# One ring of raw staging tiles from the output projection to the FFN, and the first FFN weights loaded and summed within the last attention pair

## The chip, the cores and the metric

The kernel runs on one NeuronCore of a Trainium2 chip. TensorE (PE) does the matmuls, VectorE (DVE), ScalarE (ACT) and GpSimd (POOL) the rest, and SyncE (SP) issues most of the DMA transfers; ACT issues some. The metric is the device time of one execution in microseconds (us).

## What is computed

One encoder layer on x of 2048 positions by 1024 channels, in fp32:

```python
h = _rmsnorm(x, norm_mix_g)
x = x + _hybrid_mixer(h, ...)              # gMLP, pooling and dilated attention heads, then y @ w_out
h = _rmsnorm(x, norm_mem_g)
x = x + _memory_cross_attention(h, mem_n, w_q, w_kv, w_o, b_o)   # 4 heads, 256 memory tokens
h = _rmsnorm(x, norm_ffn_g)
x = x + _conv_ffn(h, ...)                  # up to 2 x 2816, width-3 convolution, silu gate, down
return _rmsnorm(x, final_norm_g)
```

## The kernel before

**Number format.** Each fp32 operand is kept as a high part, which the matmul takes exactly, and a low part, the rest. `mm3` makes a product of three matmuls: high by high (L115), high by low (L116), low by high (L117). So each weight that is loaded must be split: one operation makes the high part (POOL in `split_w`, ACT in the FFN), one on DVE the low part.

**Stages.** The order in time is: input projection and mixer; output projection in four chunks of 512 positions (`OutProj.chunk`); cross-attention (`xattn`); FFN up for the first half of the positions (`up_half(0)`); FFN down and up for the rest.

**Output projection.** A chunk loads six `y` tiles, splits them, and for each of eight blocks d of output channels loads `xt`, does 18 matmuls into `pt`, adds on DVE (L1265), and writes x1 to DRAM. During chunks 2 and 3 the eight row blocks of the matrix `a_d` (for the logits) are loaded through staging tiles `st` and split into `am0` to `am7`. The pool of `st`, `c_st`, has two buffers.

**Cross-attention.** The eight row blocks of `vo_d` (values times output weights) go through the same two `st` buffers and are split into `vm0` to `vm7`; POOL makes the high parts (L95), DVE the low parts (L99). `logits(s)` treats 128 positions: x1 is loaded and split, 48 matmuls go into `pl`, DVE takes the maximum `mx` (L1347) and scales it to `nm`, ACT takes exponentials into `p` (L1350), POOL divides. `ssq` (L1321) is the sum of squares for the norm, which PE adds over partitions (`pr`, L74). `turn` transposes `p` on DVE (L108, 16 operations). Two such blocks are a pair: `parts` splits the transposed `p` into `ph` and `pl_`, and `pv` does, for each of eight d, 24 matmuls into `po` (two PSUM buffers), an addition on DVE (`xr`, L1400), a DMA of x2 to DRAM, a square on ACT and its addition on POOL (`sq`, in the last pair `sql`, L1407). `xr` has three buffers, and the buffer of the square only one.

**FFN.** The up product is done with seven block products instead of eight (a Strassen-like scheme): from two loaded weight tiles `wa` and `wb`, POOL makes sums and differences `ws` and `wt` with four operations (L272 to L277), and `split` makes high parts on ACT (L265) and low parts on DVE (L266). `prep(0)` makes the matching sums of the activations (`hb`) and their parts `hth`, `htl`, for four groups kk. It is a generator, advanced between the steps of the last two attention pairs; its last piece, for kk = 3, comes after the last `pv`, since the pool `f_h3` is opened only there. The FFN starts with

```python
self.w0 = self.weights(self.ORDER[0])
rest()
```

The first products are `px`, `pz` and `py`.

**What sets the order.** Each engine works its own instructions in program order and waits on semaphores. The program order on each engine is laid down when the kernel is built, by a scheduler that simulates the program; memory comes from pools, and a tile that takes over the space of an older tile waits for whatever still uses it. So a change of pools moves instructions on all engines.

Of the kernel before, what the change touches and what calls it, by code (L numbers as in the profile page):

```python
# [9 lines left out]
F32 = mybir.dt.float32  # L10
# [109 lines left out]
class Ffn:  # L120
# [13 lines left out]
    def __init__(self, cx, es, x2, w_up, b_up, conv, w_down, b_down, gn, g_fin, act, out):  # L134
# [4 lines left out]
        self.pool = cx.pools(es)  # L139
# [11 lines left out]
    def open(self):  # L151

        one = self.one = self.pool("f_one", 1, side="right")
        self.carry = one.tile([P, 2 * NF, 3], F32, name="carry")
        self.h3 = self.pool("f_h3", 1, side="right")
        self.raw = self.pool("f_raw", 5, side="right")
        self.wp = self.pool("f_w", 1, side="right")

    def prep(self, half, es):
# [37 lines left out]
        for kk in range(4):  # L197
# [29 lines left out]
            else:  # L227
                sub(dve, T1, B12, B11)
                sub(gps, T3, B22, B12)
                sub(dve, T2, B22, T1)  # L230
                yield
# [3 lines left out]
                sub(gps, T4, B21, T2)  # L235
# [8 lines left out]

    def weights(self, fa):

# [4 lines left out]

    def weight_pieces(self, fa, w):

        nc, N, raw = self.nc, self.N, self.raw
        a = raw.tile([P, 2, N], F32, name="wa", tag="raw")
        nc.sync.dma_start(a.rearrange("p a n -> p (a n)"), self.w_up[fa])
        b = raw.tile([P, 2, N], F32, name="wb", tag="raw")
        nc.sync.dma_start(b.rearrange("p a n -> p (a n)"), self.w_up[fa + 1])
        s = raw.tile([P, 2, N], F32, name="ws", tag="raw")
        t = raw.tile([P, 2, N], F32, name="wt", tag="raw")  # L260

        def split(src, prods):
            m = len(prods)
            hl = self.wp.tile([P, 2, m, N], F32R, name="w", tag=f"w{m}", bufs=4 if m == 2 else 2)
            nc.scalar.activation(hl[:, 0], src, AF.Copy)  # L265
            nc.vector.tensor_tensor(hl[:, 1], src, hl[:, 0].bitcast(F32), op=ALU.subtract)  # L266
            for j, p in enumerate(prods):
                w[p] = (hl[:, 0, j], hl[:, 1, j])

        split(a, (1, 2))  # L270
        tt = nc.gpsimd.tensor_tensor
        tt(s[:, 0], b[:, 0], b[:, 1], op=ALU.add)  # L272
        tt(s[:, 1], s[:, 0], a[:, 0], op=ALU.subtract)
        yield
        split(s, (5, 6))
        tt(t[:, 0], a[:, 0], b[:, 0], op=ALU.subtract)
        tt(t[:, 1], a[:, 1], s[:, 1], op=ALU.subtract)  # L277
        split(t, (7, 3))
        split(b[:, 1:2], (4,))
# [240 lines left out]

    def run(self, rest, sq):
# [3 lines left out]
        self.w0 = self.weights(self.ORDER[0])  # L525
        rest()

# [4 lines left out]
        with ExitStack() as e:  # L532
            pool, pst, pu = banks(e, 1)
            self.up_half(0, pu, pool, lambda: cx.rows_of(self.one, pst, sq, 2, cx.r3[:, NS - 2:], 1.0))
            for c0 in (0, N):
                pt = pst.tile([P, N], F32, name="pt", tag="pt")
                cx.spread(self.one, pt, cx.r3[:, (H + c0) // P:(H + c0 + N) // P])
                nc.scalar.activation(cx.rb[:, c0:c0 + N], pt, AF.Copy)  # L538
# [684 lines left out]
class OutProj:  # L1223


    def __init__(self, cx, late, es, eo, x_t, yt, w_out, b_out, x1_d):
        self.cx, self.x_t, self.yt, self.x1_d = cx, x_t, yt, x1_d
        pool = cx.pools(es)
        self.st = pool("c_st", 2, side="right")
# [11 lines left out]
    def load_w(self, pl, tag, src, st=None):  # L1241
        t = (st or self.st).tile([P, D], F32, name="st", tag="st")
# [28 lines left out]
def xattn(cx, proj, es, eo, a_d, vo_d, b_o, x1_d, x2_d, ffn):  # L1271
# [6 lines left out]
    with es:  # L1278
# [91 lines left out]
        def parts(pts, spare):  # L1370

            if spare:
                ph = [proj.st.tile([P, 4, N2], F32R, name="ph2", tag="st") for _ in range(2)]
                pl = [pw.tile([P, 4, N2], F32R, name="pl2", tag="pt", bufs=2) for _ in range(2)]
            else:
                ph = wk.tile([P, KD, N2], F32R, name="ph", tag="ph", bufs=1)
                pl = wk.tile([P, KD, N2], F32R, name="pl_", tag="pl_", bufs=1)
                ph, pl = ([t[:, :4], t[:, 4:]] for t in (ph, pl))  # L1380
# [43 lines left out]
        for q in range(NS // 2):  # L1424
# [6 lines left out]
            elif q == last - 1:  # L1431
# [7 lines left out]
                def each(d):  # L1439
                    if d == 2:  # L1440
                        nxt.append(turn_pe(p2))
                    if d > 1 and len(nf[0].hs) < 3:
# [98 lines left out]
```

## Time and profile before

| | us |
|---|---|
| time, median of 3 runs | 2560.48 (2557.45 to 2561.59) |
| the profiled execution, its own time | 2568.14 |
| its span, first to last instruction | 2566.3 |
| PE busy in it | 2477.1 (97%) |
| DVE, ACT, POOL busy | 1807.6, 1000.3, 959.3 |

PE is busy nearly all the time. What a change can win is mostly idle time of PE, and time in which PE ran at the lower of its two clock levels. The profiled execution is 7.7 us longer than the median.

### The profile page before, as it was taken

How to read it: one execution, taken by the hardware profiler on the slowest of the kernel's cores; microseconds unless marked ns; L12 is line 12 of the kernel's file. 1: busy time of each engine (PE TensorE's matmuls, PEld its weight loads, DVE VectorE, ACT ScalarE, POOL GpSimd, SP SyncE). 2: the span in 40 equal slices, each digit the busy share in tenths (PEclk: the TensorE clock that was granted, in tenths of full speed). 3: DMA queues.
4: the chain of work that ended last, by engine and by line, in shares of the span. 5: the costliest groups of instructions: out<-in, count | busy, mean ns of one | idle time of the engine just before them, and what ended most of it. 6: DMA issues, size and time to landing. Idle time of an engine off the chain costs nothing. (4 is left out here: it accounts for less than half of the span.)

```text
span 2566.3 us, 34002 instructions
## 1 busy us (share of the span) xinstructions
PE 2477.1 (97%) x12454; PEld 2115.8 (82%) x12454; DVE 1807.6 (70%) x2658; ACT 1000.3 (39%) x1524; POOL 959.3 (37%) x805
## 2 busy tenths in 40 slices
PE   8999997899999999998999999999999999999998
PEld 6998896898877899987888888877888887888886
DVE  6575747777655876777888888786888887645553
ACT  4122112566311333333444444453444444444442
POOL 3212314674102333346555554025565553111000
PEclk9999998899999999999999999999999999999998
DMA  9345527675663122133222223582222223867673
GB/s 300 115 141 153 152 69 222 205 235 177 195 215 122 58 68 73 52 104 110 83 74 91 82 74 107 191 266 91 84 74 83 90 74 107 277 216 240 211 233 119
DMA packets 220096, 361.59 MB, mean 141 GB/s; under 512 B 38828, under 2 KB 104472, under 8 KB 219928
## 3 DMA queue, kind: packets, MB, share of 16 engines
q1 hardware_dynamic: 155980, 286.83, 35.6%
q10 hardware_dynamic: 63948, 72.58, 8.3%
q8 instruction: 98, 1.61, 0.3%
q14 instruction: 70, 0.57, 0.1%
HBM read 280.61 MB, written 79.90 MB: 140 GB/s over the span
## 5 line engine op out<-in xcount | busy, mean ns | idle before, releaser
L403 DVE TENSOR_TENSOR w<-dr,w 128x1024 fp32r<-128x1024 f32 x176 | 220.0, 1258 | 167.4 <-ACT w L402 163.7
L116 PE MATMUL pd<-w 128*128 128x512 f32 x704 | 274.5, 390 | 1.7 <-DVE w L403 1.7
L117 PE MATMUL pd<-w 128*128 128x512 f32 x704 | 274.1, 389 | 0.0
L402 ACT ACTIVATE w<-dr 128x1024 fp32r<-128x1024 f32 x176 | 185.0, 1058 | 216.9 <-PE pd L117 198.8
L115 PE MATMUL pd<-w 128*128 128x512 f32 x704 | 259.2, 390 | 0.7 <-ACT rb L538 0.7
L116 PE MATMUL py<-htl,w 128*128 128x512 f32 x528 | 208.5, 395 | 0.0
L115 PE MATMUL py<-hth,w 128*128 128x512 f32 x528 | 207.0, 394 | 0.8 <-DVE u L371 0.8
L117 PE MATMUL py<-hth,w 128*128 128x512 f32 x528 | 206.0, 394 | 0.0
L315 DVE SCALAR_TENSOR_TENSOR t<-u,vec,t 128x1022 f32<-128x1022 f32 (+1 forms) x88 | 134.0, 1523 | 70.0 <-ACT t L314 48.1
L314 ACT ACTIVATE t<-u,vec 128x1022 f32<-128x1022 f32 (+1 forms) x88 | 109.5, 1244 | 158.3 <-DVE u L364 139.6
L116 PEld LDWEIGHTS pd<-w 128*128 128x128 f32 x704 | 132.2, 188 | 30.0 <-DVE w L403 2.8
L115 PEld LDWEIGHTS pd<-w 128*128 128x128 f32 x704 | 132.0, 188 | 27.9 <-ACT rb L538 0.9
L117 PEld LDWEIGHTS pd<-w 128*128 128x128 f32 x704 | 132.2, 188 | 27.2
L115 PE MATMUL px<-hth,w 128*128 128x512 f32 x352 | 139.9, 397 | 6.5 <-ACT w L265 4.7
L95 POOL TENSOR_SCALAR wth<-st 128x1024 fp32r<-128x1024 f32 (+1 forms) x48 | 50.0, 1042 | 257.0 <-PE pz L116 174.9
L117 PE MATMUL px<-hth,w 128*128 128x512 f32 x352 | 139.5, 397 | 3.1 <-DVE w L266 3.1
L462 POOL TENSOR_TENSOR q<-q 128x512 f32<-128x512 f32 x24 | 38.4, 1598 | 274.7 <-ACT q L458 273.4
L116 PE MATMUL px<-htl,w 128*128 128x512 f32 x352 | 140.0, 398 | 0.0
L116 PE MATMUL pz<-htl,w 128*128 128x512 f32 x352 | 139.0, 395 | 0.0
L117 PE MATMUL pz<-hth,w 128*128 128x512 f32 x352 | 138.8, 394 | 0.0
L115 PE MATMUL pz<-hth,w 128*128 128x512 f32 x352 | 138.5, 393 | 0.0
L316 DVE SCALAR_TENSOR_TENSOR t<-u,vec,t 128x1022 f32<-128x1022 f32 (+1 forms) x88 | 136.2, 1548 | 0.1
(716 smaller groups left out, 7151.8 us busy)
## 6 DMA issues: line engine op xcount, KB each, us to landing
dr<-act_d SPq DMA_DIRECT2D x176, 256.0 KB, 3.8
dr<-in_w_down_dram SPq DMA_DIRECT2D x176, 256.0 KB, 4.1
wa<-in_w_up_dram SPq DMA_DIRECT2D x44, 512.0 KB, 3.2
wb<-in_w_up_dram SPq DMA_DIRECT2D x44, 512.0 KB, 3.3
st<-in_w_t_dram SPq DMA_DIRECT2D x32, 512.0 KB, 4.0
xt<-in_x_t_dram SPq DMA_DIRECT2D x56, 256.0 KB, 4.6
act_d<-t ACTq DMA_DIRECT2D x22, 513.0 KB, 3.1
act_d<-t ACTq DMA_DIRECT2D x22, 511.0 KB, 3.0
```

The lines of the kernel that those rows point to most:

```text
L95: nc.gpsimd.tensor_scalar(hi, src, 1.0, 1.0, op0=ALU.mult, op1=ALU.mult)
L115: mm(out, a[0], b[0], start=start, stop=False, skip_group_check=again)
L116: mm(out, a[0], b[1], start=False, stop=False, skip_group_check=again)
L117: self.mm = mm(out, a[1], b[0], start=False, stop=stop, skip_group_check=again)
L314: nc.scalar.activation(t, u[:, 1:n + 1], AF.Identity, bias=vec[:, 4, f:f + 1], scale=vec[:, 2, f:f + 1])
L315: nc.vector.scalar_tensor_tensor(t, u[:, 0:n], vec[:, 1, f:f + 1], t, op0=ALU.mult, op1=ALU.add)
L316: nc.vector.scalar_tensor_tensor(t, u[:, 2:n + 2], vec[:, 3, f:f + 1], t, op0=ALU.mult, op1=ALU.add)
L402: nc.scalar.activation(hl[:, 0], t, AF.Copy)
L403: nc.vector.tensor_tensor(hl[:, 1], t, hl[:, 0].bitcast(F32), op=ALU.subtract)
L462: nc.gpsimd.tensor_tensor(sq[0], sq[0], q, op=ALU.add)
```

## The change

The ring `raw` of five buffers (each 4 KB per partition) is opened with the output projection, in place of `c_st` (two buffers), of `f_raw` (five buffers, FFN) and of the single-buffered tiles for `ph` and `pl_`. Through it go, in this order, the loads of `a_d` and `vo_d`, the parts `ph` and `pl_` of the attention pairs (four of the five buffers each), and the FFN's weights. The load of the first FFN weights and POOL's four sums are issued in the last attention pair, after its second d (`stage_first`). The two spreads of the norm's row factors into `rb`, which stood behind `up_half(0)`, are done within it (`between`). In the last pair each step of `prep` is taken one by one, in a fixed number per d.

```diff
-        self.raw = self.pool("f_raw", 5, side="right")
...
+    def load(self, tile, fa, i):
+        self.nc.sync.dma_start(tile.rearrange("p a n -> p (a n)"), self.w_up[fa + i])
+        return tile
...
+    def sums(self, a, b, s, t):
+        tt = self.nc.gpsimd.tensor_tensor
+        tt(s[:, 0], b[:, 0], b[:, 1], op=ALU.add)
+        tt(s[:, 1], s[:, 0], a[:, 0], op=ALU.subtract)
+        tt(t[:, 0], a[:, 0], b[:, 0], op=ALU.subtract)
+        tt(t[:, 1], a[:, 1], s[:, 1], op=ALU.subtract)
...
+    def stage_first(self):
+        a, b, s, t = self.staged = [self.raw.tile([P, 2, self.N], F32, name="w" + n, tag="raw") for n in "abst"]
+        self.load(a, self.ORDER[0], 0)
+        self.load(b, self.ORDER[0], 1)
+        self.sums(a, b, s, t)
...
-        self.w0 = self.weights(self.ORDER[0])
+        (a, b, s, t), self.w0 = self.staged, {}
+        self.weight_part(self.w0, a, 1, 2)
+        self.weight_part(self.w0, s, 5, 6)
         rest()
+        self.weight_part(self.w0, t, 7, 3)
+        self.weight_part(self.w0, b[:, 1:2], 4)
...
-            self.up_half(0, pu, pool, lambda: cx.rows_of(self.one, pst, sq, 2, cx.r3[:, NS - 2:], 1.0))
-            for c0 in (0, N):
-                pt = pst.tile([P, N], F32, name="pt", tag="pt")
-                cx.spread(self.one, pt, cx.r3[:, (H + c0) // P:(H + c0 + N) // P])
-                nc.scalar.activation(cx.rb[:, c0:c0 + N], pt, AF.Copy)
+            def between():
+                cx.rows_of(self.one, pst, sq, 2, cx.r3[:, NS - 2:], 1.0)
+                for c0 in (0, N):
+                    pt = pst.tile([P, N], F32, name="pt", tag="pt")
+                    cx.spread(self.one, pt, cx.r3[:, (H + c0) // P:(H + c0 + N) // P])
+                    nc.scalar.activation(cx.rb[:, c0:c0 + N], pt, AF.Copy)
+            self.up_half(0, pu, pool, between)
...
-        self.st = pool("c_st", 2, side="right")
...
-        t = (st or self.st).tile([P, D], F32, name="st", tag="st")
+        t = (st or self.cx.raw).tile([P, D], F32, name="st", tag="st" if st else "raw")
...
+            def ring(n):
+                return cx.raw.tile([P, 4, N2], F32R, name=n, tag="raw")
             if spare:
-                ph = [proj.st.tile([P, 4, N2], F32R, name="ph2", tag="st") for _ in range(2)]
-                pl = [pw.tile([P, 4, N2], F32R, name="pl2", tag="pt", bufs=2) for _ in range(2)]
+                ph = [pw.tile([P, 4, N2], F32R, name="ph", tag="p"), ring("ph")]
+                pl = [pw.tile([P, 4, N2], F32R, name="pl_", tag="pt", bufs=2) for _ in range(2)]
             else:
-                ph = wk.tile([P, KD, N2], F32R, name="ph", tag="ph", bufs=1)
-                pl = wk.tile([P, KD, N2], F32R, name="pl_", tag="pl_", bufs=1)
-                ph, pl = ([t[:, :4], t[:, 4:]] for t in (ph, pl))
+                ph, pl = ([ring(n) for _ in range(2)] for n in ("ph", "pl_"))
...
                 def each(d):
-                    if len(nf[0].hs) < 3:
+                    for _ in range((1, 1, 1, 2, 1, 1, 1, 0)[d]):
                         next(pieces)
+                    if d == 1:
+                        nf[0].stage_first()
...
+            cx.raw = late.enter_context(tc.tile_pool(name="raw", bufs=5, side="right", reuse_waits="tile"))
```

**The SP queue in the second and third chunk.** `st<-vo_d` is a load of a row block of `vo_d`, `st<-a_d` of `a_d`; `xt` are the residual tiles of the chunks and `x1` the blocks for the logits. Before:

```order
L1261 DMA xt_7234<-in_x_t_dram 128x512
L1243 DMA st_7662<-a_d_98 128x1024
L1313 DMA x1_8158<-x1_d_100 128x8x128
L1243 DMA st_7714<-a_d_98 128x1024
L1261 DMA xt_7257<-in_x_t_dram 128x512
L1243 DMA st_7766<-a_d_98 128x1024
L1261 DMA xt_7280<-in_x_t_dram 128x512
L1243 DMA st_7818<-a_d_98 128x1024
L1261 DMA xt_7372<-in_x_t_dram 128x512
L1243 DMA st_7844<-vo_d_99 128x1024
L1261 DMA xt_7395<-in_x_t_dram 128x512
L1243 DMA st_7850<-vo_d_99 128x1024
```

After, the stretch up to the same `xt_7257`:

```order
L1260 DMA st_7766<-a_d_98 128x1024
L1260 DMA st_7818<-a_d_98 128x1024
L1260 DMA st_7844<-vo_d_99 128x1024
L1260 DMA st_7850<-vo_d_99 128x1024
L1330 DMA x1_8042<-x1_d_100 128x8x128
L1260 DMA st_7856<-vo_d_99 128x1024
L1330 DMA x1_8158<-x1_d_100 128x8x128
L1278 DMA xt_7211<-in_x_t_dram 128x512
L1260 DMA st_7862<-vo_d_99 128x1024
L1260 DMA st_7868<-vo_d_99 128x1024
L1278 DMA xt_7234<-in_x_t_dram 128x512
L1278 DMA xt_7257<-in_x_t_dram 128x512
```

Five loads of `vo_d` now stand ahead of `xt_7257`; before, none did, two came later in the chunk, and the other six behind the last chunk, where three stand now. Of the eight loads of `a_d`, five instead of two are now issued during the first chunk (not shown).

**DVE in the first two logits blocks.** `mx_8123` is the maximum of the second block, `vm6l` and `vm7l` are low parts of `vo_d`, and the transposes are those of the first block. Before:

```order
L108 STREAM_TRANSPOSE pt_8025<-p_8006 32x8x32 x15
L99 TENSOR_TENSOR vm6l_7883<-st_7880,vm6h_7882 128x1024
L108 STREAM_TRANSPOSE pt_8025<-p_8006 32x8x32
L1347 TENSOR_REDUCE mx_8123<-pl_8053 128x2
L99 TENSOR_TENSOR vm7l_7889<-st_7886,vm7h_7888 128x1024
L1348 TENSOR_SCALAR nm_8124<-mx_8123,r_7936 128x2
L1385 TENSOR_TENSOR pl__8258<-pt_8025,ph_8257 128x4x128 x2
L1321 TENSOR_REDUCE ssq_8662<-sx_8661 128x128
L1352 RECIPROCAL rd_8126<-dn_8125 128x2
L1347 TENSOR_REDUCE mx_8123<-pl_8053 128x2
L1348 TENSOR_SCALAR nm_8124<-mx_8123,r_7936 128x2
```

After:

```order
L108 STREAM_TRANSPOSE pt_8025<-p_8006 32x8x32 x16
L1364 TENSOR_REDUCE mx_8123<-pl_8053 128x2
L1365 TENSOR_SCALAR nm_8124<-mx_8123,r_7936 128x2
L1403 TENSOR_TENSOR pl__8259<-pt_8025,ph_8257 128x4x128
L1403 TENSOR_TENSOR pl__8260<-pt_8025,ph_8258 128x4x128
L1369 RECIPROCAL rd_8126<-dn_8125 128x2
L1364 TENSOR_REDUCE mx_8123<-pl_8053 128x2
L1365 TENSOR_SCALAR nm_8124<-mx_8123,r_7936 128x2
L1338 TENSOR_REDUCE ssq_8664<-sx_8663 128x128
```

The splits of `vm4` to `vm7` have gone from the first two blocks: those up to `vm6l` now stand ahead of the first block's maximum, and `vm7l` right behind it.

**ACT and POOL at the start of the FFN.** The rows are those behind the last attention product; `hth` and `htl` are parts of the activations, `s1` the last square, `w_12136` and `w_12157` the parts of the first weight tile `wa`. ACT before:

```order
L182 ACTIVATE hth_12158<-hb_12152 128x512
L1401 DMA x2_d_101<-xr_12077 128x256 [waits DMAHW2_49,DVE_49]
L1406 ACTIVATE s1_12106<-xr_12077 128x256 [waits Pool_49]
L265 ACTIVATE w_12136<-wa_12130 128x1024 [waits DMAHW0_49]
L265 ACTIVATE w_12149<-wb_12132 128x512 [waits DMAHW1_49]
L265 ACTIVATE w_12141<-ws_12134 128x1024 [waits Pool_49]
```

ACT after:

```order
L181 ACTIVATE hth_12163<-hb_12069 128x512
L1419 DMA x2_d_101<-xr_12108 128x256 [waits DMAHW3_49,DVE_49]
L1424 ACTIVATE s1_12137<-xr_12108 128x256 [waits Pool_49]
L260 ACTIVATE w_12157<-wa_11911 128x1024 [waits DMAHW4_49,DMAHW3_49,DMAHW5_49,DMAHW2_49,DMAHW6_49,DMAHW1_49,DMAHW7_49,DMAHW0_49,Pool_49]
L260 ACTIVATE w_12160<-ws_11913 128x1024
L260 ACTIVATE w_12174<-wt_11914 128x1024
L260 ACTIVATE w_12177<-wb_11912 128x512
```

The first weight operation of ACT waited for the load of `wa` alone; now it waits for the last writes of x2 (the eight DMA semaphores) and for POOL's last addition of a square, since its tile `w` takes over space that `xr` and the squares used. POOL before, from the first `sql` addition on:

```order
L1407 TENSOR_TENSOR sql_11823<-sql_11823,s1_11890 128x256
L1407 TENSOR_TENSOR sql_11823<-sql_11823,s1_11926 128x256
L1407 TENSOR_TENSOR sql_11823<-sql_11823,s1_11964 128x256
L1407 TENSOR_TENSOR sql_11823<-sql_11823,s1_11999 128x256
L1407 TENSOR_TENSOR sql_11823<-sql_11823,s1_12038 128x256
L1407 TENSOR_TENSOR sql_11823<-sql_11823,s1_12074 128x256
L185 TENSOR_TENSOR htl_12159<-hb_12152,hth_12158 128x1024
L1407 TENSOR_TENSOR sql_11823<-sql_11823,s1_12106 128x256
L272 TENSOR_TENSOR ws_12134<-wb_12132 128x512
L276 TENSOR_TENSOR wt_12135<-wa_12130,wb_12132 128x512
```

POOL after:

```order
L251 TENSOR_TENSOR ws_11913<-wb_11912 128x512
L253 TENSOR_TENSOR wt_11914<-wa_11911,wb_11912 128x512
L252 TENSOR_TENSOR ws_11913<-ws_11913,wa_11911 128x512
L187 TENSOR_TENSOR hb_12069<-hb_12069 128x512
L254 TENSOR_TENSOR wt_11914<-wa_11911,ws_11913 128x512
L187 TENSOR_TENSOR hb_12069<-hb_12069 128x512
L1425 TENSOR_TENSOR sql_11838<-sql_11838,s1_11904 128x256
L1425 TENSOR_TENSOR sql_11838<-sql_11838,s1_11950 128x256
L1425 TENSOR_TENSOR sql_11838<-sql_11838,s1_11988 128x256
L1425 TENSOR_TENSOR sql_11838<-sql_11838,s1_12030 128x256
```

The four sums have gone from behind the last `sql` addition to ahead of the first one. On PE the order behind the last attention product was two matmuls of `px`, then the other ten; now it is two of `px`, two of `pz`, two of `py`, then the other ten of `px`.

On all engines other rows are in another order too: on PE the two orders part at row 2,205 of some 12,300, in the mixer's attention, and last differ at row 9,001, in the FFN; the matmuls with weights are the same in number.

## Rows read from the trace of the kernel before

**Rows 1.** The page: span, busy time of the engines, one group of matmuls.
```profile
span 2566.3 us, 34002 instructions
PE 2477.1 (97%) x12454; PEld 2115.8 (82%) x12454; DVE 1807.6 (70%) x2658; ACT 1000.3 (39%) x1524; POOL 959.3 (37%) x805
...
L115 PE MATMUL pd<-w 128*128 128x512 f32 x704 | 259.2, 390 | 0.7 <-ACT rb L538 0.7
```

**Rows 2.** The waits of PE, 625 to 1200 us: waiting line, releaser, sum, times, longest.
```profile
PE px L115 <- ACT w L265: 4.7, 1, 4.7
PE pt L1018 <- ACT yo L1070: 4.1, 1, 4.1
```

**Rows 3.** Windows: length, busy PE, PEld, DVE, ACT, POOL, PE clock, DMA share, GB/s.
```profile
831.00:838.00 7.00, 4.89 (x12) 3.94 (x13) 6.40 (x21) 2.15 (x5) 4.20 (x5) 0.51 0.00 0
1186.00:1196.00 10.00, 5.03 (x11) 3.54 (x12) 7.66 (x4) 3.36 (x6) 9.92 (x8) 0.51 0.32 110
635.00:640.00 5.00, 5.00 (x21) 4.52 (x22) 3.27 (x8) 4.80 (x15) 0.00 (x0) 0.50 0.86 259
690.00:706.00 16.00, 13.87 (x64) 11.41 (x62) 8.23 (x8) 4.64 (x5) 6.03 (x4) 1.00 0.93 263
```

**Rows 4.** Timelines, SP queue and POOL: start, length, engine, line; in brackets idle before, releaser.
```profile
796.85 8.88 SPq L1243 DMA_DIRECT2D st<-vo_d  x4
...
800.90 1.05 POOL L95 TENSOR_SCALAR vm2h<-st 128x1024 fp32r<-128x1024 f32 x1 [5.23 <-DMA st<-vo_d]
819.39 1.05 POOL L95 TENSOR_SCALAR vm7h<-st 128x1024 fp32r<-128x1024 f32 x1 [1.53 <-DMA st<-vo_d]
```

**Rows 5.** Timelines of DVE and PE, 815 to 838 us.
```profile
824.49 1.23 DVE L99 TENSOR_TENSOR vm6l<-st,vm6h 128x1024 fp32r<-128x1024 f32 x1
826.21 0.69 DVE L1347 TENSOR_REDUCE mx<-pl 128x2 f32<-128x512 f32 x1
826.93 1.22 DVE L99 TENSOR_TENSOR vm7l<-st,vm7h 128x1024 fp32r<-128x1024 f32 x1
829.40 1.86 DVE L1321 TENSOR_REDUCE ssq<-sx 128x128 f32<-128x1024 f32 x1
...
831.32 0.59 PE L74 MATMUL pr<-ones,ssq 128*128 128x2 f32 x2 [2.47 <-DVE ssq L1321]
833.69 0.79 PE L115 MATMUL pl<-am0h,hh 128*128 128x512 f32 x1 [1.78 <-ACT p L1350]
```

**Rows 6.** Timelines of ACT, POOL, DVE and PE, 1181 to 1193 us.
```profile
1186.78 1.04 ACT L265 ACTIVATE w<-wa 128x1024 fp32r<-128x1024 f32 x1
...
1181.81 0.74 POOL L1407 TENSOR_TENSOR sql<-sql,s 128x256 f32<-128x256 f32 x1 [1.81 <-ACT s L1406]
1187.14 2.24 POOL L1407 TENSOR_TENSOR sql<-sql,s 128x256 f32<-128x256 f32 x1
1191.01 2.25 POOL L276 TENSOR_TENSOR wt<-wa,wb 128x512 f32<-128x512 f32 x1
...
1186.15 3.78 DVE L185 TENSOR_TENSOR htl<-hb,hth 128x1536 fp32r<-128x1536 f32 x2 [1.19 <-ACT hth L182]
1189.85 2.28 DVE L266 TENSOR_TENSOR w<-wa,w 128x1024 fp32r<-128x1024 f32 x1
...
1192.18 0.80 PE L117 MATMUL px<-hth,w 128*128 128x512 f32 x1 [3.09 <-DVE w L266]
```

**Rows 7.** Timelines of DVE and PE in the last attention pair.
```profile
1159.82 1.85 DVE L185 TENSOR_TENSOR htl<-hb,hth 128x1536 fp32r<-128x1536 f32 x1 [0.62 <-ACT hth L182]
1170.97 0.48 DVE L1400 SCALAR_TENSOR_TENSOR xr<-po,bo,xr 128x256 f32<-128x256 f32 x1
...
1171.51 0.38 PE L115 MATMUL po<-ph,vm0h 128*128 128x256 f32 x1
```

**Rows 8.** Timelines of the SP queue and of DVE, second chunk.
```profile
704.89 0.91 SPq L1261 DMA_DIRECT2D xt<-in_x_t_dram  x2
...
724.04 0.75 DVE L1265 SCALAR_TENSOR_TENSOR xt<-pt,bo,xt 128x512 f32<-128x512 f32 x1
```

More of the change, by code (lines that the diff above doesn't have):

```diff
@@ L138, in __init__ @@
         nc = self.nc
-        self.pool = cx.pools(es)
+        self.pool, self.raw = cx.pools(es), cx.raw
         self.eh = ExitStack()
@@ L230, in prep @@
                 sub(dve, T2, B22, T1)
+                sub(gps, T4, B21, T2)
                 yield
@@ L234, in prep @@
                 low(dve, B11, B12)
-                sub(gps, T4, B21, T2)
                 high(B21, B11)
@@ L243, in prep, with weight_part, weight_pieces @@
             self.hs.append((hi, lo))
+    def load(self, tile, fa, i):
[7 more added lines that the diff above has]
+        tt(t[:, 1], a[:, 1], s[:, 1], op=ALU.subtract)
+    def weight_part(self, w, src, *prods):
+        nc, N, m = self.nc, self.N, len(prods)
+        hl = self.wp.tile([P, 2, m, N], F32R, name="w", tag=f"w{m}", bufs=4 if m == 2 else 2)
+        nc.scalar.activation(hl[:, 0], src, AF.Copy)
+        nc.vector.tensor_tensor(hl[:, 1], src, hl[:, 0].bitcast(F32), op=ALU.subtract)
+        for j, p in enumerate(prods):
+            w[p] = (hl[:, 0, j], hl[:, 1, j])
+    def weight_pieces(self, fa, w):
+        a, b, s, t = (self.raw.tile([P, 2, self.N], F32, name="w" + n, tag="raw") for n in "abst")
+        self.load(a, fa, 0)
+        self.load(b, fa, 1)
+        self.weight_part(w, a, 1, 2)
+        self.sums(a, b, s, t)
+        yield
+        self.weight_part(w, s, 5, 6)
+        self.weight_part(w, t, 7, 3)
+        self.weight_part(w, b[:, 1:2], 4)
     def weights(self, fa):
@@ L250, in weights @@
         return w
[L252 to L279, printed above, removed]
     ORDER = [f + v for f in range(0, NF, 2) for v in (0, NF)]
@@ L519, in final @@
                                                                         x3[:, d - 1:d + 1])
+    def stage_first(self):
+        a, b, s, t = self.staged = [self.raw.tile([P, 2, self.N], F32, name="w" + n, tag="raw") for n in "abst"]
+        self.load(a, self.ORDER[0], 0)
+        self.load(b, self.ORDER[0], 1)
+        self.sums(a, b, s, t)
     def run(self, rest, sq):
         cx, nc, N, H = self.cx, self.nc, self.N, self.H
-        self.w0 = self.weights(self.ORDER[0])
+        (a, b, s, t), self.w0 = self.staged, {}
+        self.weight_part(self.w0, a, 1, 2)
+        self.weight_part(self.w0, s, 5, 6)
         rest()
+        self.weight_part(self.w0, t, 7, 3)
+        self.weight_part(self.w0, b[:, 1:2], 4)
         def banks(e, n):
@@ L1441, in each @@
                         nxt.append(turn_pe(p2))
-                    if d > 1 and len(nf[0].hs) < 3:
+                    if d > 1:
                         next(pieces)
```

## Prediction

> **What bounds the kernel now.** I read the page first: PE is busy 2477.1 us of a span of 2566.3, or 97% [rows 1]. The change adds and removes no matmul of weight, so it can win only where PE waits, or where it runs at the lower of its two clock levels, 1.2 instead of 2.4 GHz. Then I read the waits of PE and the timelines around them. Three places bear on the change.
>
> At the seam into the FFN PE waits 4.7 us for the first high part of a weight [rows 2], does two matmuls, and waits 3.09 us for the low part [rows 6]. From 1186 to 1196 us the granted clock is 0.51, the lower level [rows 3].
>
> In the first logits blocks of the cross-attention PE waits 2.47 us for `ssq` and, one small matmul later, 1.78 us for ACT's exponentials [rows 5]; behind that come 7 us at a clock of 0.51 [rows 3]. What is late there is DVE: between the transposes of the first block and the second block's maximum (826.21) stands `vm6l`, and right behind that maximum `vm7l`, 1.23 and 1.22 us, since `vo_d` came late: its loads are issued one by one from 796.85 on, over 8.88 us for the first four, and the split of the last begins at 819.39 [rows 4, 5].
>
> Ahead of the output projection PE waits 4.1 us for `yo` [rows 2], and 635 to 640 us run at 0.50 [rows 3]. The order of rows there changes too.
>
> **The change part by part.**
>
> *Loads of vo_d (ring of five).* After the change three loads instead of six are left when chunk 3 ends. Each needs one buffer free, that is one low part done on DVE. By the first such load, which is issued at 796.85 and whose split starts at 800.90 [rows 4], a load takes 4.05 us to its use. Buffers come free about every 1.2 us, so the last of the three is split by about 805, before the first maximum, where it was 819.39. Then DVE has no split left between the transposes and the second block. Taking away `vm6l` (1.23) moves the maximum from 826.21 to about 824.9. From that maximum to PE's next `pl` at 833.69 there are 7.48 us of work on DVE and ACT; out of it go `vm7l` (1.22) and `ssq` (1.86, at 829.40 [rows 5]), which now stands behind the second scaling, and which PE no longer needs here: the one `pr` left is for an earlier block. So PE can go on at 824.9 + 7.48 - 1.22 - 1.86, about 829.3 instead of 833.69, which I round to 4.2 us. Then the 7 us at half clock fall away. PE was busy 4.89 us in them [rows 3], and at full clock that work takes half: 2.4 us. Sum **-6.6**. Lower bound of the gain: the 4.2 us less the 1.7 of the second wait that may stay, -2.5 with the clock still falling. Upper bound: -9, if the waits on `xr` behind these blocks shrink too, which I do not count.
>
> *Seam.* The four sums and the loads are gone from here, and two high parts come one after the other on ACT. But the first high part now waits for the last addition of a square on POOL and the last writes of x2, where it waited for `wa` alone. That addition ended at 1189.38 (1187.14 plus 2.24), while the high part had started at 1186.78 [rows 6]. Nothing in the change brings this addition forward: in front of it stands the same `htl` on POOL, and beside it the same `htl` on DVE. So the high part starts at 1189.4 instead of 1186.78, and PE's first `px` at 1190.4, 2.6 us later than before. Then it pays back: two `px`, the next high part at 1191.5, and four matmuls of `pz` and `py` cover the low part, which DVE (free from 1189.93) has done by 1191.8. PE runs without a break from about 1191.5 with two matmuls done; before, that was 1192.18 [rows 6]. Gain 0.7. If the addition took 0.74 us as the one at 1181.81 did, it would end at 1187.9, and the gain were 2.2. Taken between: **-1.3**. Bounds: +2 if the writes of x2 land 2.7 us later than the addition (the weight loads that stood beside them move away, so I hold that unlikely); -4.9 if nothing of the new wait costs (`px` at 1187.9, no break from 1189.0, 3.2 us, and one third of the stretch at half clock gone, 1.7).
>
> *Two engines, one after the other.* At 1186.15 two low parts of DVE (1536 and 512 columns) took 3.78 us [rows 6]; the larger one alone takes 1.85 [rows 7], and by its length the smaller 0.6. In the same time POOL's addition took 2.24 instead of 0.74. So when both work on SBUF they lose what the other takes. The Trainium skill says so as a rule: in the page SBUF — State Buffer, section "SBUF: two separate sides", a DVE operation with two SBUF inputs and a GpSimd operation that reads SBUF hold a shared pair of ports as an exclusive lock, whoever comes first, for the whole instruction. The trace agrees in size (3.78 is near 1.85 + 0.6 + 2.24 less the overlap at the ends). By that rule the sums do not get free by moving: they now stand in the last pair against DVE's scaling and differences there.
>
> *Last pair.* There the row that counts is the addition `xr` of the third d: it starts at 1170.97, ends at 1171.45, and PE's fifth d starts at 1171.51 [rows 7] into the buffer that this frees. So there is no slack. DVE reaches this addition after two scalings, two differences and part of a norm; POOL now has four sums beside them, of which one took 2.25 us at the seam [rows 6]. If DVE loses none of them, PE loses nothing; if it loses a whole one, 2.25, unless the stretch has some slack to catch up. I take half, **+1.2**, with 0 and +2.3 as ends. POOL's additions of squares come 3 to 4 us later, and the buffer of the square holds up ACT's next square; this delays x2 writes little, since they stand ahead of the squares on ACT. Without that cover it is the upper end.
>
> *Spreads of rb.* They go into `up_half(0)`, where PE has other work: the 0.7 us that the down product waits for `rb` [rows 1] go: **-0.7**.
>
> *Order ahead of and within the output projection.* More loads stand on SP earlier, and the scheduler laid the mixer's attention out anew. I cannot trace this row by row, so it is **0**, with bounds from the largest wait there: 4.1 us [rows 2] and the stretch of 5.0 us at half clock behind it, 2.5 [rows 3], together 6.6 either way.
>
> *Sum.* -6.6 - 1.3 + 1.2 - 0.7 + 0 = -7.4, against the span of 2566.3 (profiled execution 2568.14). The profiled execution lies 7.7 us above the median of 2560.48; the waits do not depend on that, so I take the sum off the median: 2553.1, say **2553**.
>
> **The rivals.**
>
> *A. The seam goes wholly.* Both waits and the half clock (5.03 us of work at 0.51, so 2.5) make 4.7 + 3.1 + 2.5 = 10.3 instead of 1.3: 2544. Against it: four high parts of `hth`, which wait for the end of the last product, still stand on ACT ahead of the first weight, and the new wait on POOL. Chance 0.1.
>
> *B. Hardly any net change.* The gain at the logits stays at 2.5, and the seam's new wait costs what its better order saves: -2.5 + 0 + 1.2 - 0.7 = -2, so 2558.5. For it: all these gains hang on DVE, which is 70% busy and would be late by something else. Chance 0.27.
>
> *C. Slower: the SP queue in the second chunk.* Between the residual tiles of the second chunk stand, after the change, five loads of `vo_d` of 0.52 MB that came later before. At 263 GB/s, with DMA 0.93 busy [rows 3], that is 2.6 MB or 10 us. Each also waits for a low part on DVE, and holds up whatever stands behind it on SP. The `xt` pair that was issued at 704.89 is used at 724.04 for its second tile [rows 8]. If it is issued 10 us later, it still lands in time when a load takes under 9 us; every us beyond is a wait of PE. With waits of 5 us at each of three tiles (15) the sum is -7.4 + 15, so 2568. It decides from about 9 us of delay. Against it: the `a_d` loads that stood there have moved ahead. Chance 0.13.
>
> **How the numbers follow.** The forecast has a chance of 0.5; its own range is 2549 to 2557. Below 0.2% (5.1 us) a measurement of this kernel tells little from no change. The forecast counts to 0.45 as faster and 0.05 as same, A as faster, B to 0.05 as faster and 0.22 as same, C as slower: 0.60, 0.27, 0.13. The range leaves out half of C and the far end of A: 2543 to 2565.
>
> **What would show it.** Right: no wait of PE on `ssq` or on exponentials between 826 and 834, no half clock behind; the last `vm` split ahead of the first maximum; at the seam one long wait of about 7 us in place of 4.7 and 3.1, released by ACT's first weight part, and that by POOL; no wait for `rb`. Wrong: long waits on `xt` between 690 and 730; new waits of `po` on `xr` of over 2 us in the last pair; a mixer that ends much earlier or later than 635 us.

## The result, and the profile after

The changed kernel takes 2580.60 us (median of 6 runs, 2572.09 to 2583.84), the kernel before 2559.64 us (6 runs, 2553.51 to 2562.21). The ratio is 1.008, with a 95% interval of 1.0066 to 1.0094: slower, where the forecast was 2553 and faster, and beyond the upper end of the range (2565).

The page of the changed kernel first, in the lines that answer to [rows 1].

```profile
span 2578.4 us, 34012 instructions
PE 2484.5 (96%) x12454; PEld 2121.8 (82%) x12454; DVE 1820.6 (71%) x2658; ACT 1002.9 (39%) x1524; POOL 955.7 (37%) x805
...
L115 PE MATMUL pd<-w 128*128 128x512 f32 x704 | 259.1, 390 | 0.0
```

PE does as many matmuls as before and is longer busy by 7.4 us; the rest of the longer span is idle time. The wait for `rb` (0.7 us in [rows 1]) is gone.

To see where the time went I cut both executions at the same instructions: the first matmul of the mixer's attention, the first of the output projection, the first logits of the cross-attention, its first `po`, the first `px` and the first `pd` of each half. The execution of before on record had by chance spent some 5 us more ahead of and at the start of the attention; the table takes another profiled execution of the same kernel (span 2559.0), and, for later use, three of the experiments. All in us.

| stage | before, again | padded before | after | late ring, ACT | after, 64 bytes |
|---|---|---|---|---|---|
| ahead of the mixer's attention | 424.7 | 426.1 | 423.2 | 420.1 | 427.5 |
| mixer's attention | 205.8 | 223.4 | 221.5 | 201.0 | 224.2 |
| output projection | 159.5 | 159.3 | 159.2 | 157.4 | 157.1 |
| first logits to first `po` | 51.3 | 51.5 | 46.1 | 47.8 | 47.8 |
| rest of the cross-attention, to first `px` | 340.4 | 340.6 | 351.1 | 348.1 | 348.1 |
| first up half | 438.9 | 439.3 | 435.3 | 424.8 | 424.5 |
| first down half | 123.1 | 123.4 | 125.5 | 123.6 | 124.9 |
| second up half | 431.3 | 431.5 | 431.0 | 420.1 | 420.1 |
| second down half | 373.5 | 373.8 | 375.4 | 374.2 | 374.2 |
| last matmul at | 2548.5 | 2568.9 | 2568.3 | 2517.1 | 2548.4 |

Of the 19.8 us between before and after, 15.7 lie in the mixer's attention, which the diff does not touch. The cross-attention's first stage gains 5.2, the rest of it loses 10.7, and the first up half gains 3.6.

The windows of the changed kernel, for the attention and for the second up half (columns as in [rows 3]):

```profile
423.20:644.70 221.50, 190.20 (x1325) 180.31 (x1325) 163.63 (x381) 125.44 (x356) 133.12 (x87) 0.88 0.62 194
...
1761.90:2192.90 431.00, 430.16 (x1849) 346.59 (x1850) 346.26 (x283) 193.06 (x218) 234.41 (x189) 1.00 0.25 86
```

and the same of before:

```profile
424.70:630.50 205.80, 180.03 (x1336) 170.59 (x1336) 156.87 (x393) 126.81 (x362) 135.67 (x88) 0.94 0.70 211
...
1743.70:2175.00 431.30, 430.36 (x1848) 346.67 (x1849) 345.02 (x283) 193.26 (x218) 234.03 (x189) 1.00 0.25 86
```

In the attention nearly the same number of matmuls (1325 and 1336) keeps PE busy for 190.2 instead of 180.0 us, at a granted clock (the share of the full clock that PE was given) of 0.88 instead of 0.94, and PE is idle for 31.3 instead of 25.8 us (221.5 less 190.2; 205.8 less 180.0). PE's waits from 420 to 650 us in the changed kernel:

```profile
PE pl L115 <- DVE oe L1026: 6.5, 2, 5.4
PE pt L115 <- DVE kvl L1183: 4.5, 4, 1.4
PE po L1050 <- DVE oe L1055: 3.8, 1, 3.8
PE pt L115 <- POOL kwh L95: 3.4, 1, 3.4
PE pt L1036 <- ACT yo L1088: 3.4, 1, 3.4
```

The wait for `yo` is still there (4.1 in [rows 2]); waits of 5.4, 3.8 and 3.4 us on `oe` and `kwh` are new or longer. The waits on `oe` in the other execution of before:

```profile
PE pl L115 <- DVE oe L1008: 4.3, 2, 3.7
PE po L1032 <- DVE oe L1037: 1.1, 1, 1.1
```

Behind each of the three waits the clock falls in the changed kernel; three windows show it:

```profile
462.00:472.00 10.00, 6.64 (x31) 6.65 (x32) 7.38 (x22) 5.27 (x20) 3.66 (x3) 0.50 0.62 193
486.00:493.00 7.00, 6.40 (x29) 6.23 (x29) 2.62 (x4) 1.55 (x5) 6.38 (x6) 0.52 0.87 250
595.00:605.00 10.00, 8.35 (x36) 7.98 (x37) 5.38 (x13) 2.90 (x9) 2.37 (x3) 0.50 0.66 210
```

Now the places the prediction spoke of, in the timelines of the changed kernel: first the logits blocks on POOL, DVE and PE.

```profile
801.65 1.05 POOL L95 TENSOR_SCALAR vm0h<-st 128x1024 fp32r<-128x1024 f32 x1 [82.96 <-PE pt L117]
...
809.67 2.01 POOL L95 TENSOR_SCALAR vm5h<-st 128x1024 fp32r<-128x1024 f32 x1
...
814.66 2.06 DVE L99 TENSOR_TENSOR vm6l<-st,vm6h 128x1024 fp32r<-128x1024 f32 x1
816.64 0.68 DVE L1364 TENSOR_REDUCE mx<-pl 128x2 f32<-128x512 f32 x1
817.24 2.81 DVE L99 TENSOR_TENSOR vm7l<-st,vm7h 128x1024 fp32r<-128x1024 f32 x1
...
838.96 0.50 PE L115 MATMUL pl<-am0h,hh 128*128 128x512 f32 x1 [2.07 <-ACT p L1367]
```

All splits but the last stand ahead of the first maximum. Of the two waits in [rows 5] one of 2.07 us is left, and no half clock follows it (838 to 850 us: 1.00, against 0.51 at 831 to 838 us in [rows 3]). But POOL makes the first high part only when the projection's last products release it (PE `pt`), as it did before:

```profile
793.62 1.05 POOL L95 TENSOR_SCALAR vm0h<-st 128x1024 fp32r<-128x1024 f32 x1 [66.44 <-PE pt L117]
```

So the five loads that came early lay in the ring until then, and all eight splits stand behind the last chunk. A high part on POOL now takes 2.01 us instead of 1.05 [rows 4], and a low part on DVE 2.06 instead of 1.22 [rows 5]. And the next blocks pay:

```profile
868.97 7.18 DVE L108 STREAM_TRANSPOSE pt<-p 32x256 f32<-32x256 f32 x16 [1.07 <-POOL p L1371]
876.19 0.88 DVE L1418 SCALAR_TENSOR_TENSOR xr<-po,bo,xr 128x256 f32<-128x256 f32 x2
...
885.93 0.47 DVE L1418 SCALAR_TENSOR_TENSOR xr<-po,bo,xr 128x256 f32<-128x256 f32 x1
...
886.45 0.58 PE L115 MATMUL po<-ph,vm0h 128*128 128x256 f32 x1 [3.57 <-DVE xr L1418]
```

DVE evicts PE's `po` only after 7.18 us of transposes or behind a chain of small operations, and PE waits for the buffer. Behind the longest of these waits the clock is at half:

```profile
885.00:892.00 7.00, 5.55 (x26) 5.55 (x27) 1.99 (x6) 2.87 (x7) 3.30 (x6) 0.52 0.31 100
```

From 850 us to the seam that makes 15.7 us in ten waits:

```profile
PE po L115 <- DVE xr L1418: 15.7, 10, 3.6
PE px L115 <- ACT w L260: 7.3, 1, 7.3
```

Before, the same two, from 841 us on:

```profile
PE po L115 <- DVE xr L1400: 5.3, 6, 1.8
PE px L115 <- ACT w L265: 4.7, 1, 4.7
```

Last the end of the cross-attention and the seam. Before, PE waited twice for `xr` in the last pair:

```profile
1158.74 0.36 PE L115 MATMUL po<-ph,vm0h 128*128 128x256 f32 x1 [1.45 <-DVE xr L1400]
1162.11 0.39 PE L115 MATMUL po<-ph,vm0h 128*128 128x256 f32 x1 [0.29 <-DVE xr L1400]
```

The changed kernel:

```profile
1170.36 2.01 POOL L251 TENSOR_TENSOR ws<-wb 128x512 f32<-128x512 f32 x1 [0.19 <-DMA wb<-in_w_up_dram]
1172.34 2.25 POOL L253 TENSOR_TENSOR wt<-wa,wb 128x512 f32<-128x512 f32 x1
...
1173.90 0.39 PE L115 MATMUL po<-ph,vm0h 128*128 128x256 f32 x1 [2.30 <-DVE xr L1418]
...
1196.42 4.12 DVE L184 TENSOR_TENSOR htl<-hb,hth 128x1536 fp32r<-128x1536 f32 x2 [0.83 <-ACT hth L181]
...
1197.76 2.24 POOL L1425 TENSOR_TENSOR sql<-sql,s 128x256 f32<-128x256 f32 x1
...
1200.03 1.06 ACT L260 ACTIVATE w<-wa 128x1024 fp32r<-128x1024 f32 x1 [2.88 <-POOL u L305]
...
1201.14 0.79 PE L115 MATMUL px<-hth,w 128*128 128x512 f32 x1 [7.33 <-ACT w L260]
```

At the seam PE waits once, 7.33 us, for ACT's first weight part, which starts when POOL's last addition has ended (1197.76 plus 2.24, then a memset). That is what the prediction drew.

### The profile page after: what moved, and what is told of

Same layout as the page of the kernel before. It is cut to its first block, busy times and chain, and to the rows that moved or that the text cites. A ratio compares the mean times of both kernels' runs of the same rounds, so it can differ in the third digit from the quotient of the medians.

```text
span 2578.4 us, 34012 instructions
## 1 busy us (share of the span) xinstructions
PE 2484.5 (96%) x12454; PEld 2121.8 (82%) x12454; DVE 1820.6 (71%) x2658; ACT 1002.9 (39%) x1524; POOL 955.7 (37%) x805
## 3 DMA queue, kind: packets, MB, share of 16 engines
q8 instruction: 97, 1.59, 0.2%
## 5 line engine op out<-in xcount | busy, mean ns | idle before, releaser
L117 PE MATMUL py<-hth,w 128*128 128x512 f32 x528 | 205.8, 394 | 0.0
L316 ACT ACTIVATE t<-u,vec 128x1022 f32<-128x1022 f32 (+1 forms) x88 | 109.6, 1245 | 157.4 <-DVE u L366 136.1
```

The lines of the kernel that those rows point to most:

```text
L117: self.mm = mm(out, a[1], b[0], start=False, stop=stop, skip_group_check=again)
L316: nc.scalar.activation(t, u[:, 1:n + 1], AF.Identity, bias=vec[:, 4, f:f + 1], scale=vec[:, 2, f:f + 1])
```

## The experiments

**1. Only the shift of memory.** The ring of five buffers lies for long above the output projection's tiles and pushes them down by 12,288 bytes in each partition. This kernel is before with an unused tile of that size.

```diff
         pool = cx.pools(eo)
+        self.pad = pool("o_pad", 1, side="right").tile([P, 3 * D], F32, name="pad")
         self.yp = pool("o_y", 7, side="right")
```

> The kernel before with one unused tile of 12 KB under the output projection's pools, so that these lie where the change puts them; nothing else. Its PE order in the mixer's attention is that of the changed kernel, from the cross-attention on that of before. Theory 1 (the new order of the attention, made by the shift of memory, costs): PE reaches its first output-projection matmul about 9 us later than before (645 instead of 636 us) and the time is 0.3 to 0.8% longer. Rival (the loss is made in the cross-attention and the last pair): 636 us, and a ratio within 0.2% of 1.

Measured: 2580.19 us, ratio 1.0078 (1.0066 to 1.009). A tile that nothing reads costs as much as the whole change. PE's order in the mixer's attention is that of the changed kernel row by row, and elsewhere that of before. Its attention, by window and by waits:

```profile
426.10:649.50 223.40, 188.47 (x1324) 178.37 (x1324) 169.94 (x380) 125.43 (x355) 133.62 (x87) 0.89 0.63 192
```

```profile
PE pt L115 <- DVE kvl L1165: 9.7, 5, 4.5
PE pl L115 <- DVE oe L1008: 6.4, 2, 5.2
PE po L1032 <- DVE oe L1037: 3.8, 1, 3.8
```

The two waits on `oe` are those of the changed kernel, and the clock is 0.89. In the table all stages behind the attention are those of before within 0.4 us; the part ahead of it is 1.4 us longer.

**2. The ring without the early weights.** The changed kernel, but the first FFN weights are loaded, summed and split at the FFN's start.

```diff
-        (a, b, s, t), self.w0 = self.staged, {}
-        self.weight_part(self.w0, a, 1, 2)
-        self.weight_part(self.w0, s, 5, 6)
+        self.w0 = self.weights(self.ORDER[0])
...
-                    if d == 1:
-                        nf[0].stage_first()
```

> The changed kernel with the first FFN weights loaded and summed at the start of the FFN, as before; the ring and the spreads stay. Theory 1 (order of the attention): still slower than before, by most of the change's 0.8%, at least 0.5%. Rival (POOL's sums in the last pair delay DVE, and the first weight waits longer): the ratio falls to 1.003 or less, and the last pair's waits of PE fall from 4.5 to about 2 us.

Measured: 2579.18 us, ratio 1.0074 (1.0062 to 1.0086). The early loads and sums make no difference that can be told. PE waits 7.33 us at the seam here too, and its longest wait in the last pair, 2.30 us for `xr`, is that of the changed kernel:

```profile
1173.54 0.40 PE L115 MATMUL po<-ph,vm0h 128*128 128x256 f32 x1 [2.30 <-DVE xr L1414]
...
1200.81 0.80 PE L115 MATMUL px<-hth,w 128*128 128x512 f32 x1 [7.33 <-ACT w L260]
```

So neither wait hangs on when the sums are made.

**3. The spreads of rb alone.** Before, with the spreads put into the first up half.

```diff
-            self.up_half(0, pu, pool, lambda: cx.rows_of(...))
-            for c0 in (0, N):
+            def between():
+                cx.rows_of(...)
+                for c0 in (0, N):
...
+            self.up_half(0, pu, pool, between)
```

> The kernel before with the two spreads of the factors moved into the first up half, and nothing else. By the sum: 0.7 us faster, which is within the noise (ratio 0.9995); the wait of PE for the row factors ahead of the down product is gone. A rival (the spreads and their DVE parts hold up the first up products): 1 to 3 us slower.

Measured: 2560.68 us, ratio 1.0000 (0.9991 to 1.001). The wait of 0.7 us is gone (the `pd` group shows 0.0), but the `py` products wait 0.7 us more for `u` (a tile that DVE makes from the products) instead, at the end of the same up half. The first line is of this run, the second of before; the changed kernel has the same 1.5.

```profile
L115 PE MATMUL py<-hth,w 128*128 128x512 f32 x528 | 207.1, 394 | 1.5 <-DVE u L371 1.5
...
L115 PE MATMUL py<-hth,w 128*128 128x512 f32 x528 | 207.0, 394 | 0.8 <-DVE u L371 0.8
```

The first up half takes 438.9 us, as in the second profile of before.

**4. Before once more,** for a second profile of it.

> The kernel before once more, for a second profile: how far its stages differ between two executions. If the mixer ends within 2 us of 636 us again, the 9 us by which the changed kernel is later there are its own; if it differs by 5 us or more, part of them is chance.

Measured: 2560.76 us (one execution), span 2559.0. It gives the first column of the table.

**5. The ring opened late.** The changed kernel, but `a_d` goes through two staging buffers of the output projection, as in before, and the ring is opened when that stage has closed, at the loads of `vo_d`. So the output projection's tiles lie where before has them.

```diff
         pool = cx.pools(eo)
+        self.st = pool("c_st", 2, side="right")
...
         eo.close()
+        cx.raw = late.enter_context(tc.tile_pool(name="raw", bufs=5, side="right", reuse_waits="tile"))
...
-        vm = [load_w(rv, f"vm{k}", vo_d[k * P:(k + 1) * P, :]) for k in range(8)]
+        vm = [load_w(rv, f"vm{k}", vo_d[k * P:(k + 1) * P, :], cx.raw, "raw") for k in range(8)]
```

> The changed kernel with the ring opened only after the output projection's last chunk; the loads of a_d go through two buffers within that projection's own pools, as before, so that the memory under the mixer's attention lies as before. Its PE order up to the third chunk is that of before, and behind the first logits that of the changed kernel. Theory 1 (only the shift of memory and the attention order that follows from it cost): the time of before within 0.2% (ratio 0.998 to 1.002), first output-projection matmul at 627 to 636 us, attention stretch about 206 us instead of 222. Rival (the ring's use by the attention pairs or the early sums cost): 1.004 or more.

Measured: 2542.40 us, ratio 0.9932 (0.9911 to 0.9953). PE's order in the attention is that of before again, and the stage takes 200.5 us. The whole time was expected within 0.2% of before, and is shorter, for the up halves are faster: 425.0 and 420.1 us where every kernel so far took 435 to 439 and 431 to 432.5. So this gain is not the ring's alone, and experiments 9 to 12 ask for its cause.

**6. High parts of vo_d on ACT.** The changed kernel with these eight operations on ScalarE in place of POOL.

```diff
-        return self.cx.split_w(pl, t, tag, tag, D)
+        return self.cx.split_w(pl, t, tag, tag, D, hi_eng="act" if tag[:2] == "vm" else "pool")
```

> The changed kernel with the high parts of vo_d made on ACT instead of POOL. Theory (the low parts on DVE took 2.05 instead of 1.22 us since POOL made high parts at the same time, and this delays the first maxima): the low parts take 1.2 us again, the first maximum comes 5 us earlier after the last chunk, and the time falls by 2 to 6 us against the changed kernel (ratio to before 1.0055 to 1.007). Rival (DVE's transposes bound this stage whatever comes ahead of them): the low parts are faster, the waits of po on xr stay, ratio 1.008.

Measured: 2579.51 us, ratio 1.0063 (1.0042 to 1.0084). The low parts take 1.22 us again, as this row of its timeline shows. Whether the kernel is faster can't be told: the interval takes in both the theory's range and the changed kernel's 1.0080. In its one profile the cross-attention (first logits to first `px`) takes 394.5 us, 2.7 less than in the changed kernel, and PE still waits 13.0 us for `xr` from 845 us on.

```profile
813.51 1.22 DVE L99 TENSOR_TENSOR vm2l<-st,vm2h 128x1024 fp32r<-128x1024 f32 x1
```

**7. A smaller unused tile.** Before with 4,096 bytes in place of 12,288.

> The kernel before with an unused tile of 4 KB instead of 12 KB under the output projection's pools. It gives a third order of the mixer's attention, other than before and other than with 12 KB. Theory 1a (each layout gives its own order, and the loss is one of the order): a time of its own, anywhere from 0.995 to 1.01, which does not follow the size. Rival 1b (less memory for the mixer's own tiles means more waiting): between before and 12 KB, about 1.003.

Measured: 2569.07 us, ratio 1.004 (1.0026 to 1.0054). PE's order in the attention is a third one, and this one costs about half as much. Its one profile does not show where: the attention took 209.3 us, and the part ahead of it 429.2. The rival that the loss follows the size is not excluded either, for its 1.003 lies within the interval.

**8. The late ring with the high parts on ACT:** experiments 5 and 6 together.

> The late ring with the high parts of vo_d on ACT. If the memory shift is the loss and the low parts on DVE the thing that eats the gain at the logits, this is the fastest kernel: 2 to 6 us below before (0.9975 to 0.999). If the transposes bound that stage: as the late ring, within 1 us.

Measured: 2541.36 us, ratio 0.9913 (0.9889 to 0.9936), the lowest of all; from experiment 5 it can't be told apart.

**9 to 12. What made the up halves fast.** In the up products of before, after and experiments 1 to 4, 6 and 7 a matmul starts 232.5 to 232.6 ns after the one before it; in both late rings it is 226.7 (means over some 1,500 matmuls of `px`, `py` and `pz`, worked out from their start times in the first up half). The order on PE in the up halves is the same in after and in the late ring. What differs is addresses: the late ring's weight tiles `w` and the fourth state pair (`hth` and `htl` of the fourth group kk, pool `f_h3`) lie 1,600 bytes lower, and so at 64 modulo 128 bytes, where the other three state pairs lie in all kernels; in before and after they lie at 0 modulo 128. Each experiment puts in one unused tile, which moves these tiles and leaves PE's order as it was.

```diff
         self.h3 = self.pool("f_h3", 1, side="right")
+        self.pad = self.pool("f_pad", 1, side="right").tile([P, 16], F32, name="pad")
         self.wp = self.pool("f_w", 1, side="right")
```

> The changed kernel with an unused tile of 64 bytes a partition opened between the FFN's fourth state pair and its weight tiles, nothing else: only the FFN's weight tiles move, down by 64 bytes; the order on TensorE is that of the changed kernel. Theory A (where the weight tiles lie modulo 128 bytes sets the rate of the FFN's up matmuls: 130304 is a multiple of 128 in before and after, 128704 in the late ring is not): px, py and pz start every 226.7 ns instead of 232.5, each up half 10 to 14 us shorter, the kernel 2556 to 2560 us. Rival B (another thing of the late ring makes its up halves faster, such as the place of the staging buffers or of the fourth state pair): 232.5 ns as before and 2580 us.

> The changed kernel with an unused tile of 1536 bytes a partition at the same place: the weight tiles move down by 1536 bytes, to 128768, 64 bytes from where the late ring has them and again at a multiple of 128. Theory A (alignment): 232.5 ns between the up matmuls, as in the changed kernel, 2580 us. Rival C (the region that the weight tiles lie in, by its distance to the state tiles or by what lies next to it): close to the late ring's 226.7 ns and 2556 to 2560 us.

> The late ring with its high parts on ScalarE, and the same unused tile of 64 bytes: its weight tiles move from 128704 to 128640, a multiple of 128. Theory A: the up matmuls fall back to 232.5 ns, the two up halves grow by 20 to 25 us together, and the kernel takes 2561 to 2566 us, about what the kernel before takes. Rival B: 226.7 ns as in the late ring, 2541 us.

Experiment 12 has the same line ahead of that of `f_h3`, so that both move:

> The changed kernel with an unused tile of 64 bytes a partition opened ahead of the FFN's fourth state pair, nothing else: the fourth state pair and the weight tiles both move down by 64 bytes, so that all operands of the up products start at 64 modulo 128 bytes, as in the late ring; staging buffers, carried columns and the order on TensorE stay as in the changed kernel. Theory A2 (the rate hangs on how weights and states lie to each other modulo 128 bytes): 226.7 ns between the up matmuls, up halves of some 425 and 420 us, the kernel 2557 to 2562 us. Rival B2 (the larger part of the late ring's rate comes from something else that it moved, such as its staging buffers): as with the weights alone moved, 230 to 232 ns, 2571 to 2576 us.

| kernel | `w` modulo 128 | fourth pair modulo 128 | ns, start to start | median us, ratio (interval) |
|---|---|---|---|---|
| after | 0 | 0 | 232.5 | 2580.60, 1.0080 (1.0066 to 1.0094) |
| 10: after, `w` moved by 1,536 | 0 | 0 | 232.5 | 2580.27, 1.0079 (1.0058 to 1.0100) |
| 9: after, `w` moved by 64 | 64 | 0 | 231.1 | 2573.51, 1.0060 (1.0041 to 1.0079) |
| 11: late ring on ACT, `w` moved by 64 | 0 | 64 | 228.9 | 2545.79, 0.9947 (0.9932 to 0.9962) |
| 12: after, both moved by 64 | 64 | 64 | 226.7 | 2558.10, 0.9988 (0.9976 to 1.0000) |
| 8: late ring on ACT | 64 | 64 | 226.7 | 2541.36, 0.9913 (0.9889 to 0.9936) |

Theory A, on the weights alone, falls: moving `w` gives only 1.4 of the 5.8 ns, or takes 2.2. Theory A2 stands: with all operands at 64 modulo 128 the rate of the late ring is there, and 64 bytes take 22.5 us from the changed kernel. Rival C, the region, falls with experiment 10, and rival B2, something else of the late ring, with experiment 12. Experiment 12's windows of the two up halves:

```profile
1204.70:1629.20 424.50, 423.88 (x1868) 350.65 (x1869) 352.96 (x299) 196.77 (x225) 234.85 (x192) 0.99 0.25 86
1754.10:2174.20 420.10, 419.25 (x1848) 346.99 (x1849) 349.38 (x283) 191.02 (x218) 234.25 (x189) 1.00 0.26 88
```

One group of matmuls of its first up half shows the same; the number behind the busy time is the mean of one in ns:

```profile
L116 PE MATMUL py<-htl,w 128*128 128x512 f32 x224 | 87.2, 389 | 0.0
```

and the same group of the changed kernel:

```profile
L116 PE MATMUL py<-htl,w 128*128 128x512 f32 x217 | 85.7, 395 | 0.0
```

## Why the prediction was wrong, point by point

**The step that failed** is "Order ahead of and within the output projection", put at 0, for no other reason than that it could not be traced, with bounds of 6.6 either way. It measured +15.4: the attention lost 15.7 and the output projection gained 0.3. Experiment 1 shows that it holds the whole loss (1.0078 of 1.0080), and that the cause is where the output projection's tiles lie: with an unused tile the loss comes, and with the ring opened late (5) it goes. In the built programs these tiles have the same addresses in after and experiment 1, 12,288 bytes below those in before and experiment 5. They lie in memory that the attention still uses: in before the split `y` tiles (`yh`, `yl`) lie over `ml`, `kwh` and `kwl`, in after over `kvl`, `mh`, `ml` and `kwh`. That the first instructions of the output projection therefore wait for other last readers, and the scheduler lays the attention out in another order, is the likely link; the runs show its two ends, shift and order, but not the link. The attention's own tiles keep their addresses in all these kernels, and both shifts, 12,288 and 4,096 bytes, are multiples of 128, so the offsets of experiments 9 to 12 are not the cause here.

The other terms, -7.4 together, came to nothing: the changed kernel and the padded kernel before differ by 0.4 us in their medians (2580.60 and 2580.19).

The bound was wrong in kind. It took the largest wait that was there (4.1 us and its half clock), as if a new order could only remove or double that. It made three waits of 3.4 to 5.4 us in places that had less, each with a stretch at half clock behind.

**Loads of vo_d, -6.6.** Of the two waits that the prediction named one went, with the half clock behind them, and the stage gained 5.2 us. But the next blocks gave it back: the waits of `po` on `xr` grew by 10.4 us (15.7 less 5.3), of which 3.2 are the last pair's, so about 7.2 in the pairs ahead of it, and the half clock came back at 885 us. The whole cross-attention, up to the first `px`, lost 5.5. The prediction counted with these waits only as an upper bound for the gain ("if the waits on `xr` behind these blocks shrink too"). Why they grew is argued, not shown: PE comes earlier to blocks in which DVE is busy with transposes, but the ring also lies under `ph` and `pl_` there. The 4.2 us of this term is also a slip: 833.69 less 829.3 is 4.4.

**Splits at full speed.** The prediction counted three splits behind the last chunk, 1.2 us each, done by about 805. There were eight, since the first high part waits for the end of the projection's products, loaded early or not. With high and low parts running side by side each pair took 1.98 us (814.66 less 812.68), and the first maximum came at 816.64. The last low part stands behind it already in the built order, so the sign "the last `vm` split ahead of the first maximum" could not come. The Trainium skill's rule of an exclusive lock (SBUF — State Buffer, "SBUF: two separate sides") would give an estimate of 2.27 us for a pair, the sum of 1.05 and 1.22; the trace's 1.98 is somewhat less. The prediction held the rule against 3.78 us, but with a sum that has POOL's 2.24 in it, which is itself the stretched time; with the 0.74 of such an addition alone the sum is 3.2. Experiment 6 takes the slow low parts away, and what they cost can't be told in the whole time.

**Seam, -1.3.** One wait of 7.33 us, forecast as about 7, in place of 4.7 and 3.09; with the second wait gone that is 0.5 less. The first up half is 3.6 shorter and the wait ahead of it 2.6 longer, so seam and `rb` together gain 1.0, where 2.0 were forecast. Right in mechanism, and about half in size.

**Last pair, +1.2.** The waits of `po` on `xr` in this pair grew from 1.74 us in the execution on record (1.45 and 0.29; 1.36 in the other) to 4.52 (1.50, 2.30 and 0.72): +2.8 to +3.2, beyond the upper end of 2.3, with one wait of over 2 us, which was among the signs of being wrong. But the reason given, POOL's four sums, falls: experiment 2, which takes the sums out of this pair, has 1.59, 2.30 and 0.76 at the same places. What it keeps is the ring under `ph` and `pl_` and the last state pair made in finer steps within this pair; which of the two makes the waits longer was not tried.

**Spreads, -0.7.** The wait for `rb` went, as forecast, but nothing was gained: experiment 3 shows the same time lost to a later `u` in the same up half.

**Rival C** had the sign but another mechanism, the SP queue in the second chunk. The output projection did not grow (159.2 against 159.5), so no such delay was there. What came nearest was the sign named at the end, "a mixer that ends much earlier or later than 635 us": it ended at 644.7.

## What to carry to other kernels

Where tiles of different stages share memory and a scheduler orders the work, a buffer that is held longer changes addresses, and with them the order of stages that the diff does not touch: put an unused tile of the same size into the kernel before, and look at the order and the time of that alone. Then open a long-lived ring no earlier than its first use needs. And compare the operands' offsets before reading a small difference of two kernels as the worth of an idea: here a move by 64 bytes was worth as much as the whole change had cost.

## What was not expected of the hardware

- **Rate and offsets.** The up products' matmuls of 128x512 start every 226.7 ns when the weights and all state pairs lie at 64 modulo 128 bytes (all at 0 was not run), and every 228.9, 231.1 or 232.5 ns when the weights, a quarter of the states, or both lie 64 bytes off. All products slow down, also those whose own tiles are placed as in the fast case: in experiment 9 the three unmoved state pairs and the moved weights lie as in experiment 12, and their matmuls, where the next one is of these pairs too, still start 231.0 ns apart on average. So it is not a matter of one matmul's own two operands alone; what it hangs on stays open. The granted clock is 0.99 to 1.00 in all these stretches, and the effect was seen in the up products only.
- **What is left of the change.** The late ring gains 17 to 18 us over before by the medians; the offsets alone were worth 22.5 in experiment 12. So its attention being that of before, the rest of the change (early weights, quicker `vo_d` loads, the ring itself) shows no gain in the whole time of any run. The kernel before with its FFN tiles moved by 64 bytes, which these results speak for, was not run.
- **POOL beside DVE.** A high part on POOL and a low part on DVE of 128x1024 took 2.01 and 2.06 us side by side, and 1.05 and 1.22 apart.
